# Scaled query-key scores on one core: the first transposes in twelve pieces, and stores released by TensorE's progress

## The chip, the core and the metric

The kernel runs on one core of a Trainium2 chip. A core has a matrix engine (TensorE, "PE" in the profile), a vector engine (VectorE, DVE), an activation engine (ScalarE, ACT), a general engine (GpSimd, POOL) and an engine that only waits, counts and issues transfers (SyncE, SP). Sixteen DMA engines move data between the chip's main memory (HBM) and the core's working memory. The engines run on their own and wait for each other through semaphores. The metric is the device time of one execution in microseconds; the time of a kernel is the median of its runs.

## The reference

```python
def setup_inputs():
    batch, heads, seq, dim = 8, 8, 512, 64
    return {
        "q": np.random.randn(batch, heads, seq, dim).astype(np.float32),
        "k": np.random.randn(batch, heads, seq, dim).astype(np.float32),
    }

def reference(q, k):
    scale = 1.0 / np.sqrt(q.shape[-1])
    return (np.einsum('bhqd,bhkd->bhqk', q, k) * scale).astype(np.float32)
```

There are 64 pairs of batch and head. For each the product of a 512x64 and a 64x512 matrix is wanted, times 1/8, with no softmax behind it. The inputs are 16.78 MB and the output is 67.11 MB.

## The kernel before

**Tiles and sets.** The output is cut into 16 tiles (`ALL`) of 4 MB. A tile g lies in one of four buffers, `big[g % 4]`, of 128 partitions x 2 halves x 8 rows x 512 columns. The same four buffers first receive the inputs, in four *units* (one for two batches): each unit has a load of keys and a load of queries. The transposed inputs are made in eight *sets*, one for each batch; a set feeds two tiles. `xb` holds the inputs cast to bfloat16, for three units; `kT` and `qz` hold the transposed keys and queries of two sets, so that one is used while the other is made. [...]

**Loads (SyncE and ScalarE, L68 to L81).** Unit 0's keys come in two halves, one from SyncE's queue and one from ScalarE's. The other seven loads are issued on SyncE's queue at once, and wait for nothing.

**Casts (GpSimd, L94 to L116).** GpSimd casts each load to bfloat16 in two pieces, adds one to "ready" after each load's second piece, and after each unit marks that unit's buffer as free for output by adding 16 to its "store" semaphore. Unit 3 goes where unit 0's casts were, so ahead of it GpSimd waits until set 1 has been transposed ("turned", L96).

**Transposes (VectorE, L179 to L196).** After a memset of `qz`, each set takes two key transposes (`turn_keys`, L167, the two halves of the head dimension) and four query transposes (`turn_queries`, L173). Set 0 waits for GpSimd's cast of the keys, then for that of the queries; from set 2 on a set waits until TensorE has used up the one whose place it takes. The last query transpose of set 0 adds to "set0", on which TensorE starts.

**Matmuls (TensorE, L121 to L148).** A tile has two halves (x) of eight rows (i), a matmul of 128x128 by 128x512 for each row (L142). The waits stand in the table `waits`, by (x, i): a row's accumulator must have been read by ScalarE ("act0" or "act1", and for rows 4 to 7 of the first half "freed0" or "freed1"), and ahead of row 1 of the first half the tile's output buffer must be free ("store0" to "store3"; from the fifth tile on this is the landing of the store four tiles earlier). After each four rows TensorE adds one to "pe", four to a tile. `takes` subtracts counts that have been used, so that the loop over four tiles can use the same numbers each time.

**Scaling (ScalarE, L151 to L156).** For each four rows ScalarE waits for "pe", multiplies by the scale and writes into the tile's buffer (L155). The first three chunks of a tile add to "act0" or "act1", the fourth to "out".

**Stores (SyncE, L82 to L90).** For each tile SyncE waits for "out", passes one count on to TensorE ("freed0" or "freed1", L85), and issues the store of the whole tile (L86). All stores stand on one queue behind the loads, in order. At the end SyncE waits for the last four stores.

Of the kernel before, what the change touches and what calls it, by code (L numbers as in the profile page):

```python
# [5 lines left out]
def kernel(  # L6
# [5 lines left out]
    nc = tc.nc  # L12
# [3 lines left out]
    Q = 32  # L16
    UNITS = B // 2
    G = H // 2
# [3 lines left out]
    RO = 8  # L22
    JJ = J // RO
    W = 4
    ALL = 2 * B
    SETS = 2 * UNITS
# [4 lines left out]

    names = ["ready", "zeroed", "turned", "pe", "out", "act0", "act1", "freed0", "freed1", "set0", "set1"]
    sem = {name: nc.alloc_semaphore(name) for name in names}
    load_sems = [nc.alloc_semaphore(f"load{n}") for n in range(2 * UNITS)]
    halves = [load_sems[0], nc.alloc_semaphore("load0b")]
# [17 lines left out]
    xw = xb.rearrange("p n w d e -> p n (w d e)").bitcast(f32).rearrange(  # L55
        "p n (w d) -> p n w d", d=D)
    kw = kT.bitcast(f32)
    qw = qz.bitcast(f32)

    def xf(v):  # L60
        return bigs[v].rearrange("p x i k -> p (x i k)").rearrange("p (x s c) -> p x s c", x=2, s=2)

    def slot(v, x):
        return v % SLOTS * 2 + x
# [3 lines left out]
    for s, queue in enumerate((nc.sync, nc.scalar)):  # L68
        first_load = queue.dma_start(
            out=xf(0)[:, 0, s].rearrange("p (x c) -> p x c", x=2), in_=k_0[s]  # L70
# [9 lines left out]
        nc.sync.dma_start(out=xf(v)[:, x].rearrange("p s c -> p (s c)"), in_=(k_r, q_r)[x][v]  # L80
                          ).then_inc(load_sems[n], 16)  # L81
    for g in range(ALL):  # L82
        nc.sync.wait_ge(sem["out"], g + 1)
        if g < ALL - 1:
            nc.sync.sem_inc(sem[f"freed{g // 2 % 2}"], 1)  # L85
        nc.sync.dma_start(out=out_r[g // 4, g // 2 % 2, g % 2],  # L86
                          in_=bigs[g % UNITS].rearrange("p x i k -> p x (i k)")
                          ).then_inc(store_sems[g % UNITS], 16)
# [5 lines left out]
    for v in range(UNITS):  # L94
# [3 lines left out]
        for x in range(2):  # L98
            if v or x:
                nc.gpsimd.wait_ge(load_sems[2 * v + x], 16)  # L100
            for s in range(2):
                if v == x == 0:
                    nc.gpsimd.wait_ge(halves[s], 16)
                src = xf(v)[:, x, s]
                dst = xb[:, slot(v, x)]
                if x == 0:
                    src = src.rearrange("p (w e d) -> p w e d", e=2, d=D)
                    dst = dst[:, s * J // 2:(s + 1) * J // 2].rearrange("p w d e -> p w e d")
                else:
                    src = src.rearrange("p (jj e i d) -> p jj e i d", e=2, i=RO, d=D)  # L110
# [10 lines left out]
    pe = nc.tensor  # L121
    pe.wait_ge(sem["set0"], 1)
    with pe.Fori(0, ALL // 4):
        for t in range(4):
            two, r = divmod(t, 2)
            was = (t + 3) % 4
            waits = {(0, 0): (f"act{was // 2}", was % 2 * 3 + 3), (0, 1): (f"store{t}", 16),
                     (0, W): (f"freed{was // 2}", was % 2 + 1),
                     (1, 0): (f"act{two}", 3 * r + 1), (1, W): (f"act{two}", 3 * r + 2)}
            takes = {(1, 1): (f"store{t}", 16)}  # L130
            if r == 0:
                takes |= {(0, 5): (f"act{1 - two}", 6), (0, 6): (f"freed{1 - two}", 2),
                          (1, 2): (f"set{two}", 1)}
            else:
                waits[1, 6] = (f"set{1 - two}", 1)
            every = sem | {f"store{n}": store_sems[n] for n in range(UNITS)}
            for x in range(2):
                for i in range(RO):
                    if (x, i) in waits:
                        name, count = waits[x, i]  # L140
                        pe.wait_ge(every[name], count)
                    ins = pe.matmul(out=ps[:, i], lhsT=qz[:, 2 * t + x, i], rhs=kT[:, 2 * t + x],  # L142
                                    start=True, stop=True)
                    if i % W == W - 1:
                        ins.then_inc(sem["pe"], 1)
                    elif (x, i) in takes:
                        name, count = takes[x, i]
                        ins.then_inc(every[name], -count)  # L148


    for g in range(ALL):  # L151
        for n in range(4):
            x, i = n // 2, n % 2 * W
            nc.scalar.wait_ge(sem["pe"], 4 * g + n + 1)
            freed = nc.scalar.mul(out=bigs[g % UNITS][:, x, i:i + W], in_=ps[:, i:i + W], mul=scale)  # L155
            freed.then_inc(sem["out" if n == 3 else f"act{g // 2 % 2}"], 1)  # L156

    def turn_keys(b, y):  # L160
        s = b % 2 * 2 * Q
        out = kw[2 * y * Q:2 * (y + 1) * Q, b % 2 * G:(b % 2 + 1) * G]
        if b < 2:
            out = out.rearrange("d g (m w) -> d g w m", m=Q)
        else:
            out = out.rearrange("d g (m w) -> d w m g", w=J)
        return nc.vector.transpose(  # L167
            out=out, in_=xw[s:s + 2 * Q, slot(b // 2, 0), :, y * Q:(y + 1) * Q])

    def turn_queries(b, y, h):  # L170
        s = (b % 2 * 2 + h) * Q
        d = (2 * y + h) * Q
        return nc.vector.transpose(  # L173
            out=qw[d:d + Q, b % 2 * G:(b % 2 + 1) * G, :, h * Q:(h + 1) * Q].rearrange(
                "d g i (m jj) -> d i jj m g", jj=JJ),
            in_=xw[s:s + Q, slot(b // 2, 1), :, y * Q:(y + 1) * Q].rearrange(
                "p (i jj) d -> p i jj d", i=RO))

    nc.vector.memset(qz, 0.0).then_inc(sem["zeroed"], 1)  # L179
    nc.vector.wait_ge(sem["zeroed"], 1)  # L180
    for b in range(SETS):
        if b >= 2:
            nc.vector.wait_ge(sem["pe"], 8 * (b - 1))
        if b % 2 == 0:
            nc.vector.wait_ge(sem["ready"], b + 1)
        for y in range(2):
            last = turn_keys(b, y)
            if b == 0:
                last.then_inc(sem[("act1", "freed1")[y]], (6, 2)[y])
        if b % 2 == 0:  # L190
            nc.vector.wait_ge(sem["ready"], b + 2)
        for y in range(2):
            for h in range(2):
                last = turn_queries(b, y, h)
        last.then_inc(sem["turned" if b == 1 else f"set{b % 2}"], 1)
    nc.vector.sem_inc(sem["set0"], 1)  # L196

# [29 lines left out]
```

## Time and profile before

| what | value |
|---|---|
| median of 4 runs | 200.83 us (200.70 to 200.94) |
| the profiled execution | 200.74 us |
| its span, from first to last instruction | 199.3 us, 738 instructions |
| TensorE, VectorE, ScalarE, GpSimd busy | 83.0, 99.4, 116.1, 38.8 us |
| 16 stores, each 4096 KB, issue to landing | 30.2 us median, 17.2 the least |
| first and last store issued | 35.5 and 169.1 us |

A row of the profile names the line, the engine and the operation, the tile written and the tile read with their shapes, and how many there were; then the busy time and the mean of one, and the idle time ahead of it with the engine that ended most of it. A row of slices has one digit for each fortieth of the span, in tenths of a slice. A row by stretches has the busy time of each engine (with its number of instructions), the clock that TensorE was granted, the mean share of the 16 DMA engines, and what they moved in GB/s. The time from issue to landing of a transfer includes its wait behind others on its queue.

### The profile page before, as it was taken

The numbers are of one execution on the slowest core, as the hardware profiler recorded it, in microseconds if no ns is written. First come the engines' busy times: TensorE is split into PE (matmuls) and PEld (weight loads), VectorE is DVE, ScalarE is ACT, GpSimd is POOL, SyncE is SP. The second block draws the span as 40 slices with busy tenths as digits, with TensorE's granted clock in tenths as the row PEclk, the third lists the DMA queues.
The fourth block names the chain that finished last, engine by engine and source line by source line (L and its number), as shares of the span: only waits on it lengthen the run. The fifth ranks groups of instructions, "written<-read, shape, count | busy, mean of one in ns | idle before, by whom it ended". The sixth has DMA issues, their size and how long they took to land.

```text
span 199.3 us, 738 instructions
## 1 busy us (share of the span) xinstructions
PE 83.0 (42%) x252; PEld 23.9 (12%) x256; DVE 99.4 (50%) x49; ACT 116.1 (58%) x65; POOL 38.8 (19%) x20
## 2 busy tenths in 40 slices
PE   0000076555566556455555664366667462000000
PEld 0000022111111111111111111021212020000000
DVE  4247999799699599129904980598000000000000
ACT  2000039999999949495959396949595959000000
POOL 0499999797000000000000000000000000000000
PEclk9999999999999969797978589957576969655555
DMA  6999999999999999999999999999999999999996
GB/s 208 423 464 428 424 421 421 421 405 428 434 434 434 428 428 434 434 434 424 428 434 437 433 424 428 437 431 434 424 431 437 431 434 424 428 434 424 434 437 289
DMA packets 5905, 83.90 MB, mean 421 GB/s; under 512 B 400, under 2 KB 400, under 8 KB 912
## 3 DMA queue, kind: packets, MB, share of 16 engines
q1 hardware_dynamic: 5632, 82.84, 97.7%
q10 hardware_dynamic: 272, 1.05, 1.3%
q14 instruction: 1, 0.01, 0.0%
HBM read 16.78 MB, written 67.11 MB: 421 GB/s over the span
## 4 chain that ended last, share of the span: by engine, by line
DMA 49%; ACT 25%; DVE 4%; POOL 2%; PE 2%; issue 1%; SPq 0%
DMA out_dram<-big 43%; ACT big L155 25%; DMA big<-in_q_dram 6%; DVE qz L173 4%; POOL xb L113 2%; PE ps L142 2%; SPq L85 0%
## 5 line engine op out<-in xcount | busy, mean ns | idle before, releaser
L155 ACT ACTIVATE big<-ps 128x2048 f32<-128x2048 f32 x64 | 114.8, 1907 | 51.0 <-PE ps L142 50.9
L142 PE MATMUL ps<-kT,qz 128*128 128x512 bf16 x252 | 83.0, 463 | 83.6 <-ACT big L155 27.0
L173 DVE STREAM_TRANSPOSE qz<-xb 32x1024 f32<-32x1024 f32 x32 | 64.5, 2017 | 1.5 <-POOL xb L113 1.0
L167 DVE STREAM_TRANSPOSE kT<-xb 64x1024 f32<-64x1024 f32 x16 | 31.4, 1960 | 35.0 <-PE ps L142 28.3
L142 PEld LDWEIGHTS ps<-kT,qz 128*128 128x128 bf16 x256 | 23.9, 110 | 142.2 <-ACT big L155 55.3
L113 POOL CAST xb<-big 128x2048 bf16<-128x2048 f32 x16 | 38.6, 2470 | 9.4 <-DMA big<-in_k_dram 7.5
L179 DVE MEMSET qz<- 128x4096 uint32 x1 | 3.5, 3472 | 2.9 <-PEq L74 2.9
L155 ACT ACT_TABLE_LOAD x1 | 1.3, 1283 | 2.0 <-PEq L74 2.0
L211 POOL MEMSET const-float32-0.0<- 128x1 f32 x1 | 0.1, 98 | 0.2 <-issue 0.2
L211 POOL MEMSET const-bfloat16-1.0<- 128x1 bf16 x1 | 0.1, 101 | 0.0
L211 POOL MEMSET const-uint8-127<- 128x1 uint8 x1 | 0.1, 101 | 0.0
L211 POOL MEMSET const-float32-1.0<- 128x1 f32 x1 | 0.1, 98 | 0.0
## 6 DMA issues: line engine op xcount, KB each, us to landing
out_dram<-big SPq DMA_DIRECT2D x16, 4096.0 KB, 30.2
big<-in_q_dram SPq DMA_DIRECT2D x4, 2048.0 KB, 23.9
big<-in_k_dram SPq DMA_DIRECT2D x3, 2048.0 KB, 23.9
big<-in_k_dram SPq DMA_DIRECT2D x1, 1024.0 KB, 7.2
big<-in_k_dram ACTq DMA_DIRECT2D x1, 1024.0 KB, 8.7
```

The lines of the kernel that those rows point to most:

```text
L113: cast = nc.gpsimd.tensor_copy(out=dst, in_=src)
L142: ins = pe.matmul(out=ps[:, i], lhsT=qz[:, 2 * t + x, i], rhs=kT[:, 2 * t + x], start=True, stop=True)
L155: freed = nc.scalar.mul(out=bigs[g % UNITS][:, x, i:i + W], in_=ps[:, i:i + W], mul=scale)
L167: return nc.vector.transpose(out=out, in_=xw[s:s + 2 * Q, slot(b // 2, 0), :, y * Q:(y + 1) * Q])
L173: return nc.vector.transpose(out=qw[d:d + Q, b % 2 * G:(b % 2 + 1) * G, :, h * Q:(h + 1) * Q].rearrange("d g i (m jj) -> d i jj m g", jj=J ...
L179: nc.vector.memset(qz, 0.0).then_inc(sem["zeroed"], 1)
L211: nc = _bacc.Bacc("TRN2", target_bir_lowering=False, num_devices=1)
```

## The change

VectorE makes the first set in twelve pieces rather than six. `turn_keys` takes a range of heads and `turn_queries` a range of rows. Four key pieces (two heads by one half of the head dimension) are followed by eight query pieces: four for rows 0 to 3, after which "set0" is given, and four for rows 4 to 7, after which one count is added to "act1". The key pieces add seven to "act1" where two counts on two semaphores were given. The other sets are made as before.

SyncE no longer waits for ScalarE's fourth chunk. For every tile but the last it waits until "pe" has reached 4g + 6, which TensorE gives after the first half of tile g+1; rows 4 to 7 of that half wait for ScalarE's fourth chunk of tile g. For the last tile it waits for "out". "freed0" and "freed1" are gone: ScalarE's fourth chunk adds to "act0" or "act1" as the others do, and TensorE waits for it there. A tile so gives four counts and a set eight.

```diff
     for g in range(ALL):
-        nc.sync.wait_ge(sem["out"], g + 1)
         if g < ALL - 1:
-            nc.sync.sem_inc(sem[f"freed{g // 2 % 2}"], 1)
+            nc.sync.wait_ge(sem["pe"], 4 * g + 6)
+        else:
+            nc.sync.wait_ge(sem["out"], 1)
         nc.sync.dma_start(out=out_r[g // 4, g // 2 % 2, g % 2],
...
-            waits = {(0, 0): (f"act{was // 2}", was % 2 * 3 + 3), (0, 1): (f"store{t}", 16),
-                     (0, W): (f"freed{was // 2}", was % 2 + 1),
-                     (1, 0): (f"act{two}", 3 * r + 1), (1, W): (f"act{two}", 3 * r + 2)}
+            waits = {(0, 0): (f"act{was // 2}", was % 2 * 4 + 3), (0, 1): (f"store{t}", 16),
+                     (0, W): (f"act{was // 2}", was % 2 * 4 + 4),
+                     (1, 0): (f"act{two}", 4 * r + 1), (1, W): (f"act{two}", 4 * r + 2)}
             takes = {(1, 1): (f"store{t}", 16)}
             if r == 0:
-                takes |= {(0, 5): (f"act{1 - two}", 6), (0, 6): (f"freed{1 - two}", 2),
-                          (1, 2): (f"set{two}", 1)}
+                takes |= {(0, 5): (f"act{1 - two}", 8), (1, 2): (f"set{two}", 1)}
...
-            freed.then_inc(sem["out" if n == 3 else f"act{g // 2 % 2}"], 1)
+            freed.then_inc(sem["out" if (g, n) == (ALL - 1, 3) else f"act{g // 2 % 2}"], 1)
...
+    def turn_keys(b, y, heads=slice(0, G)):
         s = b % 2 * 2 * Q
         out = kw[2 * y * Q:2 * (y + 1) * Q, b % 2 * G:(b % 2 + 1) * G]
+        src = xw[s:s + 2 * Q, slot(b // 2, 0), :, y * Q:(y + 1) * Q]
         if b < 2:
-            out = out.rearrange("d g (m w) -> d g w m", m=Q)
+            out = out[:, heads].rearrange("d g (m w) -> d g w m", m=Q)
+            src = src.rearrange("p (g w) d -> p g w d", g=G)[:, heads]
...
+    def turn_queries(b, y, h, rows=slice(0, RO)):
...
+    nc.vector.wait_ge(sem["ready"], 1)
+    for n in range(2):
+        for y in range(2):
+            last = turn_keys(0, y, slice(2 * n, 2 * n + 2))
+    last.then_inc(sem["act1"], 7)
+    nc.vector.wait_ge(sem["ready"], 2)
+    for n in range(RO // W):
+        for y, h in sides:
+            last = turn_queries(0, y, h, slice(n * W, (n + 1) * W))
+        last.then_inc(sem[("set0", "act1")[n]], 1)
+    for b in range(1, SETS):
```

More of the change, by code (lines that the diff above doesn't have):

```diff
@@ L30 @@
     bf16 = mybir.dt.bfloat16
-    names = ["ready", "zeroed", "turned", "pe", "out", "act0", "act1", "freed0", "freed1", "set0", "set1"]
+    names = ["ready", "zeroed", "turned", "pe", "out", "act0", "act1", "set0", "set1"]
     sem = {name: nc.alloc_semaphore(name) for name in names}
@@ L155 @@
             freed = nc.scalar.mul(out=bigs[g % UNITS][:, x, i:i + W], in_=ps[:, i:i + W], mul=scale)
-            freed.then_inc(sem["out" if n == 3 else f"act{g // 2 % 2}"], 1)
-    def turn_keys(b, y):
+            freed.then_inc(sem["out" if (g, n) == (ALL - 1, 3) else f"act{g // 2 % 2}"], 1)
+    def turn_keys(b, y, heads=slice(0, G)):
         s = b % 2 * 2 * Q
         out = kw[2 * y * Q:2 * (y + 1) * Q, b % 2 * G:(b % 2 + 1) * G]
+        src = xw[s:s + 2 * Q, slot(b // 2, 0), :, y * Q:(y + 1) * Q]
         if b < 2:
-            out = out.rearrange("d g (m w) -> d g w m", m=Q)
+            out = out[:, heads].rearrange("d g (m w) -> d g w m", m=Q)
+            src = src.rearrange("p (g w) d -> p g w d", g=G)[:, heads]
         else:
             out = out.rearrange("d g (m w) -> d w m g", w=J)
-        return nc.vector.transpose(
-            out=out, in_=xw[s:s + 2 * Q, slot(b // 2, 0), :, y * Q:(y + 1) * Q])
-    def turn_queries(b, y, h):
+        return nc.vector.transpose(out=out, in_=src)
+    def turn_queries(b, y, h, rows=slice(0, RO)):
         s = (b % 2 * 2 + h) * Q
@@ L173, in turn_queries @@
         return nc.vector.transpose(
-            out=qw[d:d + Q, b % 2 * G:(b % 2 + 1) * G, :, h * Q:(h + 1) * Q].rearrange(
+            out=qw[d:d + Q, b % 2 * G:(b % 2 + 1) * G, rows, h * Q:(h + 1) * Q].rearrange(
                 "d g i (m jj) -> d i jj m g", jj=JJ),
             in_=xw[s:s + Q, slot(b // 2, 1), :, y * Q:(y + 1) * Q].rearrange(
-                "p (i jj) d -> p i jj d", i=RO))
+                "p (i jj) d -> p i jj d", i=RO)[:, rows])
+    sides = [(y, h) for y in range(2) for h in range(2)]
     nc.vector.memset(qz, 0.0).then_inc(sem["zeroed"], 1)
     nc.vector.wait_ge(sem["zeroed"], 1)
-    for b in range(SETS):
+    nc.vector.wait_ge(sem["ready"], 1)
[9 more added lines that the diff above has]
+    for b in range(1, SETS):
         if b >= 2:
@@ L186 @@
         for y in range(2):
-            last = turn_keys(b, y)
-            if b == 0:
-                last.then_inc(sem[("act1", "freed1")[y]], (6, 2)[y])
+            turn_keys(b, y)
         if b % 2 == 0:
             nc.vector.wait_ge(sem["ready"], b + 2)
-        for y in range(2):
-            for h in range(2):
-                last = turn_queries(b, y, h)
+        for y, h in sides:
+            last = turn_queries(b, y, h)
         last.then_inc(sem["turned" if b == 1 else f"set{b % 2}"], 1)
```

## The prediction

> **What bounds the kernel now.** I read the page's slices first, then its queues, then the stores' own rows, and last the chain of waits, because a chain can name an engine that only happened to release a transfer which then stood in a queue.
>
> ```profile
> span 199.3 us, 738 instructions
> ...
> DMA  6999999999999999999999999999999999999996
> GB/s 208 423 464 428 424 421 421 421 405 428 434 434 434 428 428 434 434 434 424 428 434 437 433 424 428 437 431 434 424 431 437 431 434 424 428 434 424 434 437 289
> ...
> q1 hardware_dynamic: 5632, 82.84, 97.7%
> ...
> HBM read 16.78 MB, written 67.11 MB: 421 GB/s over the span
> ```
>
> Every slice between the first and the last has the 16 DMA engines at nine tenths or more, and SyncE's queue fills 97.7% of their time. No compute engine is over 58%. The answer by stretches says the same with a mean:
>
> ```profile
> core 0: us, PE busy (x) PEld busy (x) DVE busy (x) ACT busy (x) POOL busy (x), PEclk, DMA share, GB/s
> 70.00:195.00 125.00, 55.81 (x156) 15.92 (x159) 45.73 (x24) 73.02 (x41) 0.00 (x0) 0.74 1.01 431
> 20.00:38.00 18.00, 8.78 (x28) 2.64 (x28) 17.86 (x10) 9.81 (x6) 17.48 (x8) 1.00 0.99 423
> 42.00:70.00 28.00, 16.06 (x60) 4.73 (x61) 23.76 (x13) 28.00 (x17) 6.43 (x3) 1.00 1.01 432
> ```
>
> The DMA share (second number from the right) is 0.99 to 1.01 in loads, in early stores and in late ones. So the time is bytes over rate. The last load is issued at 5.85 and lands 37.1 later, at 42.95; the first store is issued at 35.47 and lands 17.2 later, at 52.67; the last lands at 199.2. That is (199.2 - 52.67) / 15 = 9.77 us a store, and 4.19 MB at 431 GB/s is 9.73. Nothing is lost between stores, and the first lands 9.72 after the last load, so nothing is lost between loads and stores either. The chain must be read with that in mind:
>
> ```profile
> 28.19 28.43 ACT big L155 x16
> 56.63 0.02 issue
> 56.64 0.02 SPq L85
> 56.66 0.04 issue
> 56.71 25.19 DMA out_dram<-big
> 81.90 0.45 issue
> ```
>
> It puts 28 us on ScalarE, but the store that those activations released took 25.19 us to land, of which 9.77 are its own; it stood 15.4 us behind others. ScalarE is on the chain without setting the time.
>
> The number that decides is therefore the **cover** of each store: how long before the queue runs dry it is issued. A transfer's first packets show some 1.1 us after its issue (first issue 0.73, packets from the half microsecond after 1.5), and its landing follows its last packets by about 1.0 (last packets near 198.2, landing 199.2). So a store must be issued some 2.1 us before its predecessor lands. For the first store that is 42.95 - 2.1 = 40.9; it is issued at 35.47, cover 5.4. For the second 52.67 - 2.1 = 50.6 against 42.55, cover 8. Later ones are issued 30 us before they land: cover 30.2 - 9.8 - 2.1 = 18.
>
> **The change, part by part.**
>
> *The first set in pieces.* Two key and four query transposes become four and eight of half the size. These rows give the price of a whole one, and where TensorE starts:
>
> ```profile
> 12.91 4.10 DVE L167 STREAM_TRANSPOSE kT<-xb 64x1024 f32<-64x1024 f32 x2 [6.54 <-POOL xb L113]
> 18.05 8.11 DVE L173 STREAM_TRANSPOSE qz<-xb 32x1024 f32<-32x1024 f32 x4 [1.04 <-POOL xb L113]
> 26.29 3.57 PE L142 MATMUL ps<-kT,qz 128*128 128x512 bf16 x8 [26.29 <-DVE qz L173]
> ```
>
> A whole piece is 2.03 to 2.05 us. No row shows half of one. Halving gives 1.01 if nothing is fixed. [...] The other end is 2.03, if a piece cost the same whatever its size. [...]
>
> Keys: 12.91 + 4 x 1.05 = 17.1, still under the wait for the query cast (18.05), so free. Queries: first four 18.05 + 4.2 = 22.25, last four 26.45 (before: 26.18). TensorE starts near 22.4 in place of 26.29, 3.9 earlier, but its rows 4 to 7 wait for the last four, until 26.55. ScalarE has its first chunk at 22.4 + 1.9 = 24.3 (the first four matmuls took 1.88). Its second comes at 26.55 + 1.9 = 28.45, and from there chunks start 1.77 apart (23.11 / 13), so tile 0 is done at 28.45 + 2 x 1.77 + 1.89 = 33.9; before it was 35.44. Of the 3.9 us, 1.5 remain.
>
> *When SyncE stores.* It waited for ScalarE's last chunk of tile g. Now it waits until TensorE has finished the first half of tile g+1. Rows 4 to 7 of that half wait for the same chunk, so the store comes later by at least four matmuls, 1.04 us (the groups of four in the timeline). Store 0: 33.9 + 1.1 = 35.0, against 35.47 before; cover 5.9. Store 1: 35.0 + 7.1 = 42.1, cover 8.5. Store 2 is queued behind tile 3's row 1, which waits for GpSimd's cast of unit 3. That cast waits for set 1, 0.3 later than now: row 1 goes from 48.53 to about 48.8, and the half is done near 51; it must be issued by 62.4 - 2.1 = 60.3, cover 9. From tile 6 on, row 1 of tile g+1 waits for store g-3 to land, so store g is now behind a landing. Tile 6 ends at 80.9, store 3 lands at 81.90, TensorE starts 0.45 later and needs some 2.7 for the rest of the half: issue near 85.1 in place of 80.97, 4.1 later. Store 5 lands at 70.87 + 30.6 = 101.4, so it must be issued by 99.3: cover 14. Behind SyncE's wait stand only later stores and the four final waits, whose own releases come later still. Store 15 still goes on ScalarE's last chunk (169.1), 20 us before its predecessor lands. All 15 delays lie under queued transfers: 0. Without that cover each would cost its delay, 15 x 1.1 = 16 us up to 15 x 4.1 = 62.
>
> *The counts dropped.* SyncE no longer passes the "freed" count on; TensorE waits for ScalarE. Waits through SyncE were 0.77 us where those on ScalarE directly were 0.73, so 0.04 a tile, under the same transfers: 0. The 15 increments on SyncE are gone, also 0.
>
> **Sum.** Profiled execution 200.74 (span 199.3 and 1.44 around it): start 0, stores 0, tail 0, so 200.74. The median of the runs stands 0.09 above it; I forecast 200.8. A difference under about 0.2%, 0.4 us, is what a measurement here can't tell from no change.
>
> **What could still be gained or lost at the hand-over.** From loads to stores one stretch looks thin:
>
> ```profile
> 38.00:40.00 2.00, 1.27 (x6) 0.31 (x4) 0.57 (x1) 2.00 (x2) 1.26 (x1) 1.00 1.15 475
> 40.00:42.00 2.00, 1.05 (x5) 0.31 (x4) 1.95 (x1) 2.00 (x2) 2.00 (x2) 1.00 0.88 303
> 42.00:44.00 2.00, 1.04 (x4) 0.31 (x4) 1.99 (x2) 2.00 (x2) 2.00 (x2) 1.00 1.08 459
> ```
>
> The share averages 1.04 over the six microseconds, so the engines weren't idle. In bytes the middle row is 2 x (431 - 303) / 431 = 0.6 us short, some of it packets under way. I bound it at a gain of 0.5 and a loss of 0.5, and take 0, because the store's issue moves only within a time in which the loads are still queued.
>
> **Rivals.**
>
> *A, no change* (80%): as above, 200.8, own range 200.4 to 201.2.
>
> *B, the hand-over or the loads get faster* (9%): the loads run at 423 against 431 later, and the thin stretch is real. For it: those rows. Against it: the first store moves 0.5 us in a queue that is 5 deep. [...] Time 200.3.
>
> *C, slower: the first store misses the end of the loads* (5%). Pieces cost much more than half. Once a piece passes 1.29 the keys run past 18.05, and store 0 goes out at 12.91 + 12p + 8.55. It reaches 40.9 at p = 1.62, from which the queue runs dry. At p = 2.03 it is 45.8: 4.9 us lost, 205.6. For it: no row of a half piece. Against it: a fixed part of 1.2 us would be needed, more than half of the 2.03 that a whole piece takes.
>
> *D, a small loss* (6%): later issue in a full queue turns out to cost something per store that no row shows, 0.04 each (the difference of 9.77 and 9.73) over 16 stores, 0.6: 201.4.
>
> *The change does not do what it says*: TensorE would not start before 26 us, because a wait other than "set0" holds it. Then store 0 goes at 36.6, still 4.3 before its limit: the time is A's and it is counted there.
>
> **How the numbers follow.** B gives faster 0.09, C and D slower 0.11, A same 0.80. A's own range alone would hold the time 8 times in 10; the bounds of the hand-over, 0.5 on both sides, are taken in: 200.3 to 201.3. That covers B and stops short of D's 201.4 and of C.
>
> **What the profile after would show.** Right: DMA slices of 9 throughout; the store landings 9.77 apart; first matmul at 22.4, and a gap before row 4; the first store issued at 35.0 and landing near 52.7; stores from tile 6 on some 26 us from issue to landing in place of 30; key pieces of 64x512 and query pieces of 32x512 at 1.0 to 1.1. Wrong: a DMA slice under 9 between 38 and 55 us, a first landing past 53, pieces over 1.6, or another rate with the same issue order.

## The result: 200.51 us, and where the 0.3 us went

The changed kernel takes 200.51 us (median of 38 runs, 200.42 to 200.67) against 200.82 (58 runs, 200.67 to 201.17). The ratio is 0.9984, 95% interval 0.998 to 0.9989: 0.31 us less, under the 0.2% below which the forecast called it no change, but clear of zero. The profiled execution takes 200.43 us with a span of 199.1; before it was 200.74 with 199.3.

The page of the changed kernel, in the lines that answer to those shown of before (span, busy tenths of the DMA engines in 40 slices, what they moved, the queues):

```profile
span 199.1 us, 729 instructions
...
DMA  6999999999999999999999999999999999999997
GB/s 209 443 441 431 425 421 421 421 405 428 431 431 438 431 428 428 428 441 431 423 431 431 436 434 421 431 435 434 434 425 431 434 431 434 425 428 434 421 425 323
...
q1 hardware_dynamic: 5632, 82.84, 97.8%
...
q14 instruction: 2, 0.02, 0.0%
```

And by the stretches used before (engines' busy time, then granted clock, DMA share and GB/s):

```profile
70.00:195.00 125.00, 59.99 (x157) 16.69 (x159) 46.56 (x24) 74.17 (x41) 0.00 (x0) 0.68 1.01 431
20.00:38.00 18.00, 10.46 (x28) 2.85 (x28) 17.80 (x13) 10.73 (x6) 17.48 (x8) 1.00 0.99 423
42.00:70.00 28.00, 16.89 (x60) 5.01 (x61) 22.94 (x13) 26.87 (x16) 7.14 (x3) 0.94 1.01 431
```

The DMA engines are as full as before, at the same 431, 423 and 431 GB/s (432 in the last row before). The pieces and the early start stand in the timeline:

```profile
12.88 4.45 DVE L170 STREAM_TRANSPOSE kT<-xb 64x512 f32<-64x512 f32 x4 [6.51 <-POOL xb L114]
18.06 8.90 DVE L175 STREAM_TRANSPOSE qz<-xb 32x512 f32<-32x512 f32 x8 [0.73 <-POOL xb L114]
22.61 1.87 PE L142 MATMUL ps<-kT,qz 128*128 128x512 bf16 x4 [22.61 <-DVE qz L175]
24.51 1.88 ACT L155 ACTIVATE big<-ps 128x2048 f32<-128x2048 f32 x1 [21.26 <-PE ps L142]
27.02 3.59 PE L142 MATMUL ps<-kT,qz 128*128 128x512 bf16 x8 [2.54 <-DVE qz L175]
28.94 3.65 ACT L155 ACTIVATE big<-ps 128x2048 f32<-128x2048 f32 x2 [2.55 <-PE ps L142]
32.80 16.20 ACT L155 ACTIVATE big<-ps 128x2048 f32<-128x2048 f32 x9 [0.21 <-PE ps L142]
35.80 23.11 SPq L87 DMA_DIRECT2D out_dram<-big  x4
```

TensorE starts 3.7 us earlier, yet the first store is issued at 35.80, which is 0.33 later than before, and lands at 52.9 instead of 52.67 (its 17.1 us are the least of the changed kernel's stores):

```profile
DMA to landing us min/median/max: 17.1/26.1/29.8
```

So whatever saved 0.31 us, it was not an earlier first store. Two parts can be told from the runs. The span averages 199.19 us in 40 runs of the changed kernel and 199.29 in 49 of the kernel before, taken beside the experiments: 0.10 less, with a standard error of 0.02. The larger part is **the time around the span**: the device time less the span is 1.33 us on average in the changed kernel (1.27 to 1.39) and 1.53 in the kernel before (1.39 to 1.72).

The one thing that either trace has behind the span is a packet of the DMA engines, on the queue that the profile calls "instruction". This is the DMA answer of the kernel before for 199.5 to 202 us (40 slices of 0.06 us; queue: packets, MB, share of 16 engines):

```profile
DMA  0000000000000000030000000000000000000000
...
DMA packets 1, 0.01 MB, mean 3 GB/s; under 512 B 0, under 2 KB 0, under 8 KB 0
...
q14 instruction: 1, 0.01, 0.9%
```

and this is the changed kernel, the same stretch first, and then 94 to 96 us:

```profile
DMA packets 0, 0.00 MB, mean 0 GB/s; under 512 B 0, under 2 KB 0, under 8 KB 0
```

```profile
DMA packets 52, 0.84 MB, mean 422 GB/s; under 512 B 0, under 2 KB 0, under 8 KB 0
...
q1 hardware_dynamic: 51, 0.84, 98.6%
q14 instruction: 1, 0.01, 1.0%
```

An 8 KB packet of the instruction queue comes at 200.62 us before, 1.4 us after the last instruction. In the changed kernel there is none there, and one more in the middle of the run, at 95.1. (A second packet, near 110.8, is in both.) The changed kernel has six VectorE transposes more (55 VectorE records against 49). That gave the **code theory**: with a longer VectorE program the packet moves during the run rather than after it, and the device time falls. That the packet is a block of code is the author's reading; no trace shows what it holds. The first four runs below test three others: the *first-set theory* (the early start brings the gain), the *later-store theory* (a store with fewer stores queued ahead of it moves faster) and the *count theory* (the 15 increments gone from SyncE bring it).

### The profile page after: what moved, and what is told of

Its sections match the earlier page's. It is cut to its first block, busy times and chain, and to the rows that moved or that the text cites. A ratio compares the mean times of both kernels' runs of the same rounds, so it can differ in the third digit from the quotient of the medians.

```text
span 199.1 us, 729 instructions
## 1 busy us (share of the span) xinstructions
PE 89.6 (45%) x252; PEld 25.1 (13%) x256; DVE 100.4 (50%) x55; ACT 117.0 (59%) x65; POOL 38.8 (20%) x20
## 3 DMA queue, kind: packets, MB, share of 16 engines
q10 hardware_dynamic: 272, 1.05, 1.3%
## 4 chain that ended last, share of the span: by engine, by line
DMA 56%; DVE 10%; POOL 7%; PE 7%; ACT 3%; issue 2%; POOLq 0%
DMA out_dram<-big 50%; DVE qz L175 9%; POOL xb L114 7%; PE ps L142 7%; DMA big<-in_q_dram 6%; ACT big L155 3%; DVE kT L170 1%; POOLq L117 0%; POOLq L98 0%
## 5 line engine op out<-in xcount | busy, mean ns | idle before, releaser
L142 PE MATMUL ps<-kT,qz 128*128 128x512 bf16 x252 | 89.6, 497 | 77.1 <-ACT big L155 25.3
L175 DVE STREAM_TRANSPOSE qz<-xb 32x1024 f32<-32x1024 f32 (+1 forms) x36 | 65.2, 1811 | 1.2 <-POOL xb L114 0.7
L170 DVE STREAM_TRANSPOSE kT<-xb 64x1024 f32<-64x1024 f32 (+1 forms) x18 | 31.7, 1760 | 34.3 <-PE ps L142 27.6
L142 PEld LDWEIGHTS ps<-kT,qz 128*128 128x128 bf16 x256 | 25.1, 116 | 141.1 <-ACT big L155 57.4
## 6 DMA issues: line engine op xcount, KB each, us to landing
out_dram<-big SPq DMA_DIRECT2D x16, 4096.0 KB, 26.1
```

Source lines behind the costliest of these rows:

```text
L170: return nc.vector.transpose(out=out, in_=src)
L175: return nc.vector.transpose(out=qw[d:d + Q, b % 2 * G:(b % 2 + 1) * G, rows, h * Q:(h + 1) * Q].rearrange("d g i (m jj) -> d i jj m g", j ...
```

## The experiments

**The pieces alone.** The change's transposes, with "out", "freed" and the stores as before:

```diff
...
     for g in range(ALL):
-        if g < ALL - 1:
-            nc.sync.wait_ge(sem["pe"], 4 * g + 6)
-        else:
-            nc.sync.wait_ge(sem["out"], 1)
+        nc.sync.wait_ge(sem["out"], g + 1)
+        if g < ALL - 1:
+            nc.sync.sem_inc(sem[f"freed{g // 2 % 2}"], 1)
...
-        last.then_inc(sem[("set0", "act1")[n]], 1)
+        last.then_inc(sem[("set0", "freed1")[n]], n + 1)
```

> The first set in twelve pieces alone; stores and counts as in the kernel before. My forecast's step says that the pieces cost nothing and bring nothing: 200.8 us, 0.0 against before. If the 0.31 us come from the early start (first-set theory): 200.5. If they come from the later stores or from the counts: 200.8.

Measured: 200.56 us against 200.82, ratio 0.9988 (0.9982 to 0.9995). The gain is here. Time less span is 1.33, the extra packet is at 95.65 us and none is behind the span.

**The stores and counts alone.** The changed kernel with the first set in six pieces:

```diff
-    for n in range(2):
-        for y in range(2):
-            last = turn_keys(0, y, slice(2 * n, 2 * n + 2))
-    last.then_inc(sem["act1"], 7)
+    for y in range(2):
+        last = turn_keys(0, y)
+    last.then_inc(sem["act1"], 8)
...
-    for n in range(RO // W):
-        for y, h in sides:
-            last = turn_queries(0, y, h, slice(n * W, (n + 1) * W))
-        last.then_inc(sem[("set0", "act1")[n]], 1)
+    for y, h in sides:
+        last = turn_queries(0, y, h)
+    last.then_inc(sem["set0"], 1)
```

> The stores released by TensorE and the freed counts gone; the first set in six pieces as before. First-set theory: 200.8 us. Later-store theory (a store issued with fewer stores queued ahead of it moves faster, by some 0.03 us each) and count theory (the 15 increments on SyncE gone): 200.5, with landings 9.74 apart instead of 9.77.

Measured: 200.82 against 200.82, ratio 0.9999 (0.9991 to 1.0008). The first store is issued at 36.59, the median store 26 us before it lands, and it costs and brings nothing, as the forecast had it. Fifteen instructions less on SyncE leave the packet behind the span, at 200.49, and time less span at 1.57.

**Late stores, counts kept.** The kernel before with one more wait:

```diff
             nc.sync.sem_inc(sem[f"freed{g // 2 % 2}"], 1)
+            nc.sync.wait_ge(sem["pe"], 4 * g + 6)
```

> The kernel before with one wait added: SyncE still waits for the fourth chunk and passes the freed count on, and then waits until TensorE is past the first half of the next tile before it stores. Later-store theory: 200.5 us, as the changed kernel. Count theory and first-set theory: 200.8. If all three explanations are wrong and 0.3 us belong to what surrounds the span (fewer semaphores), 200.8 with the same span as before.

Measured: 200.83, ratio 1.0 (0.9992 to 1.0009), packet at 200.61. The later-store theory, by which a shorter queue moves faster, falls with this and the last run.

**Later still.** The changed kernel, stores held to the end of the next tile:

```diff
-            nc.sync.wait_ge(sem["pe"], 4 * g + 6)
+            nc.sync.wait_ge(sem["pe"], 4 * g + 8)
```

> The changed kernel with each store but the last held until TensorE is through the whole of the next tile (count 4g+8), some 4 us later again. Later-store theory: as fast as the changed kernel or faster, 200.2 to 200.5 us, stores some 22 us from issue to landing. Count theory and first-set theory: 200.5. The first store is then issued near 39.4, still ahead of the limit of 40.9 that the forecast gave; if that limit is too late, a loss shows here.

Measured: 200.74 against 200.82, ratio 1.0003 (0.9995 to 1.0011; two of the 13 runs took over 201.3). Time less span is 1.34, as in the changed kernel, but the span averages 199.5 over 13 runs (199.2 to 200.0) where the changed kernel has 199.19. So 0.3 us are lost inside the span. The first store went out at 40.19, 0.7 ahead of the limit of 40.9 that the forecast had put. The profiled execution was the quickest one, and its trace shows no loss at the first store, which lands at 52.29, earlier than in the changed kernel. It does show a lower rate later: 427 GB/s from 100 to 150 us and 429 from 150 to 195, where the changed kernel has 431 in both. What the slower executions lose, and where, is not shown.

**Two tiles late.** The cover taken away:

```diff
-            nc.sync.wait_ge(sem["pe"], 4 * g + 6)
+            nc.sync.wait_ge(sem["pe"], min(4 * g + 10, 4 * ALL))
```

> The changed kernel with each store held for one more tile (count 4g+10, for the last two waits 64). The first store is then issued near 43, 2.1 us after the limit of 40.9 that the forecast gave, and 2.8 after the 40.2 at which the run with 4g+8 had begun to lose; all later stores keep a cover of some 4 us. Cover theory: 202.6 to 203.3 us, all of the loss ahead of the first landing, and landings 9.77 apart afterwards. If late issue costs something for each store: more, and landings further apart.

Measured: 203.73 (4 runs), ratio 1.0147 (1.0131 to 1.0162), above the expectation. By stretches (DMA share and GB/s at the right):

```profile
40.00:42.00 2.00, 1.28 (x6) 0.31 (x4) 1.72 (x1) 1.91 (x2) 2.00 (x1) 1.00 0.81 344
42.00:44.00 2.00, 1.05 (x5) 0.33 (x6) 1.99 (x2) 2.00 (x3) 2.00 (x2) 1.00 0.00 0
44.00:46.00 2.00, 1.27 (x6) 0.42 (x7) 1.99 (x2) 2.00 (x2) 2.00 (x2) 1.00 0.94 393
```

This is the dry queue. The last packets of the loads end between 41.9 and 42.3, the first store is issued at 43.28, its first packet comes at 44.18, and it lands at 54.58, 1.7 later than in the changed kernel. The rest of the loss comes afterwards: the landings are (202.17 - 54.58) / 15 = 9.84 apart instead of (199.03 - 52.9) / 15 = 9.74, another 1.5 us. The queue does not run dry again, but it moves less: 425, 428 and 427 GB/s from 55 to 100, 100 to 150 and 150 to 195 us, where the changed kernel has 431 in all three. So stores issued this late ran about 1% slower all along; why was not tried.

**Spare instructions instead of the change.** The kernel before, its transposes untouched, with tiny memsets that nobody waits for:

```diff
+    spare = nc.alloc_sbuf_tensor("spare", [P, 16], f32)[:]
...
     nc.vector.sem_inc(sem["set0"], 1)
+    for n in range(6):
+        nc.vector.memset(spare[:, n:n + 1], 0.0)
```

> The kernel before, unchanged in its transposes, with six tiny memsets of a spare tile at the end of VectorE's program (near 139 us), which nobody waits for. The traces show one 8 KB packet of the instruction queue at 200.62 us, after the span, in the kernel before, and none there but a second one at 95 us in the changed kernel; time less span is 1.53 us before and 1.33 after. Code theory (a longer VectorE program has its next block fetched during the run and not after it): 200.56 us, time less span 1.33, no packet after the span. First-set theory (the early start brings it): 200.82 and the packet stays.

Measured: 200.61 against 200.85, ratio 0.9988 (0.9982 to 0.9995). Time less span is 1.32. The DMA answer for 133 to 136 us shows where the packet went:

```profile
DMA packets 78, 1.27 MB, mean 423 GB/s; under 512 B 0, under 2 KB 0, under 8 KB 0
...
q1 hardware_dynamic: 77, 1.26, 98.8%
q14 instruction: 1, 0.01, 0.6%
```

**Three, and one.** The same with `range(3)` and `range(1)`:

> As the last, with three spare memsets. Code theory: 200.56 us or 200.82, by whether the boundary lies within three instructions; the packet after the span and the time less span have to go together. First-set theory: 200.82.

Measured: 200.58 against 200.85, ratio 0.9988 (0.9981 to 0.9995); packet at 133.3, time less span 1.33.

> The kernel before with one spare memset at the end of VectorE's program, to find the boundary. Code theory: 200.60 us with the packet inside the span and time less span at 1.33 if one instruction is enough; 200.83 with the packet near 200.6 if two or three are needed. Either way packet and time less span go together.

Measured: 200.56 against 200.86, ratio 0.9985 (0.9978 to 0.9992); packet at 174.3, time less span 1.33. One instruction of no use is enough, although the packet comes 35 us after VectorE has run it (at 138.85). The answer for 174 to 175 us:

```profile
q1 hardware_dynamic: 29, 0.48, 113.6%
q14 instruction: 1, 0.01, 1.9%
```

**Ten pieces.** The changed kernel with whole key pieces, so four instructions more on VectorE:

```diff
-    for n in range(2):
-        for y in range(2):
-            last = turn_keys(0, y, slice(2 * n, 2 * n + 2))
+    for y in range(2):
+        last = turn_keys(0, y)
```

> The changed kernel with the keys in two whole pieces and the queries in eight: the same early start (first matmul near 22.5), four instructions more than before on VectorE where the changed kernel has six. First-set theory: 200.5 us. Code theory: 200.5 with the second packet inside the span, or 200.8 with it after the span, by where the boundary lies; the early start is shown to be worth nothing if it is the latter.

Measured: 200.53, ratio 0.9985 (0.9978 to 0.9991), packet at 94.96, time less span 1.33. Since the boundary turned out to lie at one instruction, this run could not part the two theories.

**Six on GpSimd.** The same memsets on another engine:

```diff
+    spare = nc.alloc_sbuf_tensor("spare", [P, 16], f32)[:]
...
         nc.gpsimd.sem_inc(store_sems[v], 16)
+    for n in range(6):
+        nc.gpsimd.memset(spare[:, n:n + 1], 0.0)
```

> The kernel before with the same six spare memsets on GpSimd (near 48 us) in place of VectorE. If it is VectorE's own program whose last block is fetched late: 200.83 us, packet near 200.6, time less span 1.55. If any longer program or the total length does it: 200.60.

Measured: 200.87 against 200.86, ratio 0.9999 (0.9991 to 1.0008), time less span 1.60. The answer for 199.5 to 202 us has the packet where the kernel before has it:

```profile
DMA packets 1, 0.01 MB, mean 3 GB/s; under 512 B 0, under 2 KB 0, under 8 KB 0
...
q14 instruction: 1, 0.01, 0.8%
```

So it is not the length of the whole program, and six instructions on GpSimd do not do what one on VectorE does; nor did fifteen waits more or fifteen increments fewer on SyncE (late stores with counts kept, and stores and counts alone). Of the programs that were lengthened, only VectorE's mattered. Those of TensorE and ScalarE were not tried.

| kernel | VectorE records more than before | extra packet at, us | time less span, us | ratio |
|---|---|---|---|---|
| stores and counts alone | 0 | 200.5 | 1.57 | 0.9999 |
| late stores, counts kept | 0 | 200.6 | 1.54 | 1.0 |
| six on GpSimd | 0 | 201.1 | 1.60 | 0.9999 |
| one spare | 1 | 174.3 | 1.33 | 0.9985 |
| three spare | 3 | 133.3 | 1.33 | 0.9988 |
| six spare | 6 | 134.4 | 1.32 | 0.9988 |
| ten pieces | 4 | 95.0 | 1.33 | 0.9985 |
| pieces alone | 6 | 95.7 | 1.33 | 0.9988 |
| the change | 6 | 95.1 | 1.33 | 0.9984 |
| later still | 6 | 95.0 | 1.34 | 1.0003 |
| two tiles late | 6 | 97.4 | 1.32 | 1.0147 |

The last two lose their time inside the span. That the device time goes with the end of the late packet can be read from the four traces that have one. All times but the device time are counted from the first instruction:

| kernel | span ends, us | packet, us | device time, us | device time less span's end | packet's end less device time |
|---|---|---|---|---|---|
| before | 199.26 | 200.62 to 200.98 | 200.74 | 1.48 | 0.24 |
| stores and counts alone | 199.15 | 200.49 to 201.06 | 200.82 | 1.67 | 0.24 |
| late stores, counts kept | 199.26 | 200.61 to 200.97 | 200.73 | 1.47 | 0.24 |
| six on GpSimd | 199.42 | 201.05 to 201.36 | 201.12 | 1.70 | 0.24 |

In these four the distance of the device time from the packet's end is the same to a hundredth of a microsecond, while its distance from the span's end differs by 0.23. In the eight traces with no late packet the device time stands 1.32 to 1.35 behind the span's end.

## Why the forecast was right, and what it had not seen

200.8 was forecast with a range of 200.3 to 201.3, "same" at 80%. The median is 200.51, in the range and within 0.2%, though on its lower half and with an interval that leaves out zero.

**The bound held.** DMA shares of 0.99 to 1.01 and the same rates in each stretch; landings 9.74 us apart against 9.77 (the traces with spare memsets, which change nothing here, have 9.74 to 9.79).

**The step that failed** is the first line of the sum: "Profiled execution 200.74 (span 199.3 and 1.44 around it): start 0, stores 0, tail 0". The 1.44 was carried over as if nothing in the change could touch it. It is not a constant: it scatters from 1.39 to 1.72 in the kernel before, 1.53 to 1.59 on average, and it is 1.32 to 1.34 on average with any kernel here whose VectorE program is longer. That is 0.2 to 0.26 of the 0.31 us. The line's other step, an unchanged span, was off by the 0.1 that is left. The change's other instructions were costed one by one for their time, but the program's length was left out, though the page of before has a row for the instruction queue and its trace has the packet behind the span. The forecast also held that a difference under 0.2% can't be told from no change: with 58 and 38 runs, 0.16% is clear of zero.

**What the early start is worth.** The one spare memset reaches 0.9985 (0.9978 to 0.9992) with no early start, and the change 0.9984 (0.998 to 0.9989). By the ratios, what is left for all the rest of the change is not told from nothing. The spans, which leave the packet out, show up to 0.1 us: 199.19 for the change, 199.20 and 199.23 for ten pieces and pieces alone, against 199.28 to 199.29 before and 199.26 to 199.29 with spare memsets (each mean to 0.01 or 0.02). But the stores alone, without an early start, also have 199.22. What shortens the span stays open.

**The pieces** cost 1.10 each (starts 1.11 apart), where the forecast's sums have 1.05:

```profile
L175 DVE STREAM_TRANSPOSE qz<-xb x8: 1094/1098/1106, 18.1 to 25.9; 32x512 f32<-32x512 f32 x8
```

No run shows the 1.05; the runs showed 1.10 for a half piece where a whole one took 2.03, so 2 x 1.10 - 2.03 = 0.17 us did not halve (an estimate from the two rows). TensorE accordingly started at 22.61 and not 22.4, and its second four at 27.02 and not 26.55. The six whole pieces took 4.10 + 8.11 = 12.2, so twelve cost 12 x 1.05 - 12.2 = 0.4 more by the forecast's 1.05, and 12 x 1.10 - 12.2 = 1.0 by the pieces as they ran. VectorE's busy time rose from 99.4 to 100.4. Set 0 was done 0.8 later than before, and tile 3's row 1, forecast 0.3 later, came 0.7 later (49.24). All of it lay under the cover.

**The first store** was forecast for 35.0 and came at 35.80, later than before and not earlier. 0.5 of that are the pieces. The other 0.3 is a wrong spacing: chunks were put 1.77 apart as in the steady stretch, but after its wait of 2.54 us TensorE took 3.59 us for eight matmuls (3.57 for its first eight before, 1.04 for four later on), so that ScalarE's chunks came 1.9 apart and idled 0.21 ahead of the fourth. Why the eight took longer than later ones is not shown; the granted clock was 1.00 there. The cover of 5 us hid it all.

**The later stores**: store 2 near 51 forecast, 51.76 found; store 6 near 85.1, found 85.25; "some 26 us" to landing, 26.1 found. Costing them at nothing was right, by two runs that made them late alone.

**The limit of the first store**, 40.9, was about right. Issued at 43.28, the store leaves the queue dry for 1.9 us; with its first packet 0.9 after its issue and the loads' last packets ending at 41.9 to 42.3, the limit in that trace is 41.0 to 41.4. Issued at 40.19, it leaves no gap. The 0.3 us lost in that run are not shown to come from the first store, since all its stores are later.

**The rivals.** TensorE did start on "set0", at 22.61, so the change does what it says. B, a quicker hand-over from loads to stores, gave a number near the result (200.3) for a reason that is not seen: the rows at 423 and 431 GB/s did not move. C did not happen; a piece is far from 1.62. D, a small loss for each late store, is nothing with a cover of 14 us, but the run two tiles late shows it real with a cover of 4, at 0.1 us a store. The cover alone does not tell when it comes: in the trace of the run in between, 431 GB/s stood until 100 us, and the 427 came behind that, on stores with a cover of 11.

## What to carry to other kernels

In a kernel whose transfer queue is full from end to end, read for each transfer how long before the queue runs dry it is issued. Edits well inside that cover were free here (a median store issued 26 us before its landing rather than 30, with 200.82 and 200.83 us against 200.82), and the limit could be worked out to about a microsecond from issues and landings (40.9 against 41.0 to 41.4). Stores issued closer to it lost a little without the queue running dry (425 to 428 GB/s against 431 with a cover of 4 us). In such a kernel a difference of 0.1 or 0.2% is not necessarily in the work: compare device time less span (1.33 against 1.53 here), and look at the instruction queue behind the last instruction, before a reason is sought inside. A control that adds idle instructions tells an edit's purpose from its side effect.

## What the runs showed of the hardware

Of the 8 KB packets on the queue that the profile calls "instruction", one came at a time that went with the length of VectorE's program. With the VectorE program of the kernel before, it came 1.3 to 1.6 us after the last instruction of the span (200.5 to 201.1, four traces); with one to six instructions more, between 95 and 174 us (eight traces). The late packet went with 0.2 to 0.26 us more device time outside the span, and with more scatter (device time less span 1.39 to 1.72 against 1.27 to 1.40). In the four traces that have it, the packet's end and the device time differ by the same 0.24 us, while the device time less the span's end goes from 1.47 to 1.70. What the packet holds, for which engine it is, and whether anything waits for it, no trace shows. That it goes with VectorE's program is argued from the runs with spare memsets: six on VectorE moved it from 200.6 to 134.4 us, six on GpSimd left it at 201.1.

What sets the time of the packet stays open. In the five traces with pieces it came 0.8 to 1.3 us after the start of the same VectorE transpose (94.32 in the changed kernel), with ten pieces as with twelve, so the number of instructions ahead does not decide alone. With three or six spare memsets at the program's end it came at 133 to 134 us, and with one at 174, 35 us after VectorE's last instruction in the trace.

Stores of 4 MB held until the count 4g + 10 moved at 425 to 428 GB/s from 55 to 195 us, without a gap between them. Held until 4g + 8 they moved at 427 to 431, and in the ten other traces at 429 to 432.
